# Rounding the turned products of the FFNs later and in a fixed order, bias rows issued earlier, upper token parts first, in a two-layer decoder trunk

## The chip, the cores and the metric

One core of one Trainium2 chip. The metric is the device time of one execution in microseconds (us); a kernel's time is the median of several runs. An engine has its own queue and works through it in order: PE (TensorE, matrix products), DVE (VectorE), ACT (ScalarE), POOL (GpSimd); SP (SyncE) here only issues DMAs.

## The reference

Two layers over 256 tokens of width 1024, batch 1, float32. Each layer has an FFN, a token mixer and another FFN. The first mixer is a gated linear recurrence, the second an attention with forget gates, whose keys, values and gates are made from the stream after the first layer. Cut to what matters here:

```python
def swiglu(x, w_gate, w_up, w_down):
    return (jax.nn.silu(x @ w_gate) * (x @ w_up)) @ w_down      # 1024 -> 2816 -> 1024

f = swiglu(rms_norm(h, ffn1_pre_g[layer]), ffn1_w_gate[layer], ffn1_w_up[layer], ffn1_w_down[layer])
h = h + 0.5 * rms_norm(f, ffn1_post_g[layer])
...
logits = logits + c[:, :, q0:end, None] - c[:, :, None, :end]   # c: running sum of log forget gates
```

There are four FFNs. In order of time they are called the first (first layer, ahead of the mixer), second (first layer, behind it), third (second layer, ahead of the attention) and fourth FFN here.

## The kernel before, in words

**Split operands.** To keep float32 accuracy, every operand of a large product is held as two parts: an upper part rounded by ACT (an activation with Copy into `fp32r`) and a lower part, the rest, subtracted by DVE. A product is then three matmuls: upper x upper, upper x lower, lower x upper (`mm3`, L183 to L185). For weights the parts are `whi` (L173) and `wlo` (L177), for tokens `xhi` and `xlo`, for the hidden activations of an FFN `hhi` (L527) and `hlo` (L528).

**Units and slots.** The weights come in units of 512 KB (1024 numbers in each of 128 partitions): one DMA on SP's queue into one of five `raw` buffers, one `whi` and one `wlo` into one of nine pairs of buffers. The 256 tokens are two halves of 128. A slot is one unit for one half: six matmuls of 512 columns. The first half runs some units ahead of the second (four in the middle of an FFN, eight at its end); a pair of weight buffers is free again when the second half has used it. Matmul results lie in four banks (`mm`).

**An FFN** has 66 units: 5 column blocks of 512 with 4 units of the gate and 4 of the up weights each, 4 units that hold both for the last 256 columns, and 22 units of the down weights. `proj_items` makes the units of the column blocks, `pair_items` the four mixed ones, `row_items` those of the down projection, which holds two banks for each half of the tokens.

**The path of a product.** When a half is done with an up block, ACT has `sil` (silu of the gate, L498) and DVE multiplies the up bank with it into `prod` (L507), which sets that bank free. There are 12 products in an FFN: ten of 512 columns, numbers 1 to 10, and two of 256, numbers 11 and 12. The down projection needs them with the hidden columns on the partitions, so each is turned: POOL copies `prod` into `pl` with the upper and the lower 16 bits of each number apart (L510), a DMA on SP's queue turns these 16-bit halves back into `prod`'s buffer (`hidden_T`, L517), POOL joins them into `pl` (L522), then ACT and DVE make `hhi` and `hlo` from `pl` (`parts`, L527 and L528). `prod` and `pl` have two buffers each.

**What sets the order.** PE's order is written out by hand. A step that is to come some slots later is put off with `defer(n, ...)`, which counts slots. For the other engines the framework sets the order by a schedule of its own; an instruction handed to `keep_in_program_order` stays where the program has it among those that are pinned so.

**The bias rows.** For the attention, the running sums of the forget gates (`crows` in DRAM, 16 heads x 256 keys) are spread over 128 partitions. For the second block of queries that is put together in DRAM (`bias1d`): `bias_rows(0)` issues on POOL's queue one transfer of 1 MB from DRAM to DRAM for the first 128 keys (`key_rows`, L952); then four times a quarter of the heads for the other 128 keys is loaded (`bp`, L952), masked on POOL (L948) and stored (`bias_part`, L969). All this is tied to the units of the third FFN by `ahead`, from 18 units before its end on.

Of the kernel before, what the change touches and what calls it, by code (L numbers as in the profile page):

```python
# [9 lines left out]
F32 = mybir.dt.float32  # L10
# [3 lines left out]
AF = mybir.ActivationFunctionType  # L14
ALU = mybir.AluOpType
AX = mybir.AxisListType

P = 128
# [7 lines left out]
NH = 16  # L26
# [17 lines left out]
def trunk_kernel(ctx: ExitStack, tc: tile.TileContext, A: dict, out: bass.AP):  # L44
    nc = tc.nc
# [28 lines left out]
    def tensor_work(n):  # L74
        pace["t"] += n * 0.445e-3
# [5 lines left out]
    def defer(n, fn):  # L81
        pend.append([n, fn])
# [98 lines left out]
    def mm3(ps, xh, xl, wh, wl, first, last):  # L181
        tensor_work(3 * wh.shape[1])
        nc.tensor.matmul(ps, xh, wh, start=first, stop=False)  # L183
        nc.tensor.matmul(ps, xh, wl, start=False, stop=False)  # L184
        nc.tensor.matmul(ps, xl, wh, start=False, stop=last)  # L185
# [205 lines left out]
    def proj_items(w, c0, nn, get_x, post, nk=8):  # L391

        kper = min(1024 // nn, 4)
        acc = {}

        for k0 in range(0, nk, kper):
            kn = min(kper, nk - k0)

            def fetch(k0=k0, kn=kn, pieces=1):
                return load_raw(w[k0 * P:(k0 + kn) * P, c0:c0 + nn].rearrange("(k p) n -> p k n", p=P), P, kn * nn, pieces)  # L400

            def prep(fetch=fetch, kn=kn):
                return split(fetch(), P, kn * nn)

            def work(t, u, k0=k0, kn=kn, i=len(items)):
                if i < OPEN:
                    if k0 + kn == nk:
                        post(t, first_acc[t][:, :nn])
                    return
                if k0 == 0:  # L410
                    acc[t] = mmbank()
                ps = acc[t][:, :nn]
                for j in range(kn):
                    k = k0 + j
                    mm3(ps, *get_x(t, k), u.hi[:, j * nn:(j + 1) * nn], u.lo[:, j * nn:(j + 1) * nn], k == 0, k == nk - 1)
                if k0 + kn == nk:
                    post(t, acc[t][:, :nn])
            if len(items) < OPEN:
                first_loads.append(fetch)
            items.append((prep, work))  # L420
# [54 lines left out]
    def ahead(i, fn):  # L475

        prep, work = items[i]

        def both():
            fn()  # L480
            return prep()
        items[i] = (both, work)

    def ffn_items(pool_of, wg, wu, wd, post_g, next_dests, last=False, normed=False):
# [17 lines left out]
        def post_up(c0, nn):  # L502
            def f(t, ps):
                hh, hl = hid_tiles(t)
                s = sil[t][:, :nn]
                pr = pool_of().tile([P, 512], F32, tag="prod", name=nm("prod"), bufs=2)
                nc.vector.scalar_tensor_tensor(pr[:, :nn], ps, rs[t][:, 0:1], s, ALU.mult, ALU.mult)  # L507
                halves = hpool.tile([P, 512], F32, tag="t1", name=nm("pl"), bufs=2).bitcast(U16)[:, :2 * nn]
                turned = pr.bitcast(U16)[:, :2 * nn].rearrange("p (a b) -> p a b", b=P)
                nc.gpsimd.tensor_copy(halves.rearrange("p (h f) -> p h f", h=2),  # L510
                                      pr[:, :nn].bitcast(U16).rearrange("p (f h) -> p h f", h=2))
                defer(1, lambda: hidden_T(halves, turned, hh, hl))

            def hidden_T(halves, turned, hh, hl):

                m, k0 = nn // P, c0 // P
                nc.sync.dma_start(turned, halves, transpose=True)  # L517
                hv = hh[:, k0:k0 + m, :].rearrange("p a b -> p (a b)")
                lv = hl[:, k0:k0 + m, :].rearrange("p a b -> p (a b)")

                def join():
                    nc.gpsimd.tensor_copy(halves.rearrange("p (f h) -> p h f", h=2),  # L522
                                          turned.rearrange("p (h a) b -> p h (a b)", h=2))

                def parts():
                    x = halves.bitcast(F32)
                    nc.scalar.activation(hv, x, AF.Copy)  # L527
                    nc.vector.tensor_tensor(lv, x, hv.bitcast(F32), ALU.subtract)  # L528
                defer(3, join)
                defer(6, parts)  # L530
            return f

        i0 = len(items)
# [417 lines left out]
    def key_rows(v, h0, nh, k):  # L951
        tc.keep_in_program_order(nc.gpsimd.dma_start(v, kv["rows"][h0:h0 + nh, k * P:(k + 1) * P].partition_broadcast(P)))  # L952
# [2 lines left out]

    def bias_rows(i):
        def f():
            if i == 0:
                key_rows(kv["bias1"][:, :, :P], 0, NH, 0)
            v = parts_of_bias[i] = pools["f"].tile([P, 512], F32, tag="sil", name=nm("bp"), bufs=2).rearrange(  # L960
                "p (a b) -> p a b", a=4)
            key_rows(v, 4 * i, 4, 1)
        return f
# [142 lines left out]
    for g in range(4):  # L1106
# [3 lines left out]
    ffn_items(lambda: pools["f"], A["ffn1_w_gate"][1], A["ffn1_w_up"][1], A["ffn1_w_down"][1], A["ffn1_post_g"][1],  # L1110
              std_dests(GI[("mix", 1)]))
    n_ffn3 = len(items)
    for i in range(4):
        ahead(n_ffn3 - 18 + 4 * i, bias_rows(i))
        ahead(n_ffn3 - 15 + 4 * i, bias_part(i))
# [340 lines left out]
```

## Time and profile before

| | |
|---|---|
| median of 3 runs | 994.34 us (993.0 to 996.06) |
| the profiled execution's own time | 991.57 us |
| its span, first to last instruction | 989.9 us |
| mean granted clock of TensorE | 0.992 |
| moved by DMA | 196.83 MB, 199 GB/s in the mean |
| read from HBM | 182.32 MB |

Busy time of an engine is the time in which its instructions ran, not counting those that issue DMAs or set registers. In a list of waits, "A <- B: total, times, longest" says how long A's engine stood still ahead of A until B had released it. In a timeline, each row has the start in us from the span's beginning, the duration, the engine, the line, the operation and the tiles it writes and reads, and in brackets how long the engine was idle before it and what ended that. PEld is the loading of weights into TensorE, which runs beside the matmuls. A line number is that of the kernel before; the changed kernel has the same statements five to six lines further down where the diff has added lines.

### The profile page before, as it was taken

To read this page: it belongs to the slowest core of one execution; us is meant where nothing else is said; L and a number is where in the kernel's file an instruction comes from. 1 tells how busy PE (TensorE), PEld (TensorE's weight loads), DVE (VectorE), ACT (ScalarE), POOL (GpSimd) and SP (SyncE) were. 2 spreads that over 40 slices of the span, in tenths; PEclk is the share of its full clock that TensorE was granted. 3 is DMA by queue.
4 is the path that set the end of the run, shared out by engine and by line. 5 is a ranking of instruction groups with operands and counts; after the bars stand their busy time and mean duration, and the time that the engine had idled before them with its cause. 6 is when DMAs were issued, how large, how long until landed. Compare 5 with 4: busy or idle time off the path is not lost. (4 is left out here: it accounts for less than half of the span.)

```text
span 989.9 us, 13061 instructions
## 1 busy us (share of the span) xinstructions
PE 963.7 (97%) x4687; PEld 800.0 (81%) x4687; DVE 627.9 (63%) x849; ACT 522.1 (53%) x749; POOL 201.7 (20%) x206
## 2 busy tenths in 40 slices
PE   9999979999999999999999999996999999999997
PEld 6888868888888888878899888875887788888785
DVE  6758655578997665554686455554487876565642
ACT  7546434558986554443565344433366865444431
POOL 2613230000001223330102132334020012323300
PEclk9999999999999999999999999997999999999999
DMA  8687876475437867766589578777764368777631
GB/s 290 209 265 206 262 225 206 137 210 164 127 107 226 227 191 224 221 212 207 117 218 297 160 216 208 222 222 230 219 222 140 107 193 234 203 215 237 209 123 43
DMA packets 142646, 196.83 MB, mean 199 GB/s; under 512 B 58798, under 2 KB 81686, under 8 KB 142454
## 3 DMA queue, kind: packets, MB, share of 16 engines
q1 hardware_dynamic: 139782, 188.96, 64.6%
q0 software_dynamic: 2192, 6.51, 2.2%
q8 instruction: 37, 0.61, 0.3%
q10 hardware_dynamic: 608, 0.53, 0.2%
q14 instruction: 27, 0.22, 0.1%
HBM read 182.32 MB, written 3.16 MB: 187 GB/s over the span
## 5 line engine op out<-in xcount | busy, mean ns | idle before, releaser
L177 DVE TENSOR_TENSOR wlo<-raw,whi 128x1024 fp32r<-128x1024 f32 (+5 forms) x329 | 414.0, 1272 | 159.1 <-ACT whi L173 156.1
L173 ACT ACTIVATE whi<-raw 128x1024 fp32r<-128x1024 f32 (+5 forms) x329 | 338.0, 1042 | 201.1 <-PE mm L185 137.9
L183 PE MATMUL mm<-whi,xhi 128*128 128x512 f32 (+1 forms) x768 | 300.0, 391 | 0.0
L185 PE MATMUL mm<-whi,xlo 128*128 128x512 f32 (+1 forms) x768 | 298.3, 388 | 0.3 <-DVE xlo L228 0.3
L184 PE MATMUL mm<-wlo,xhi 128*128 128x512 f32 (+1 forms) x768 | 298.3, 388 | 0.0
L183 PEld LDWEIGHTS mm<-whi,xhi 128*128 128x128 f32 x768 | 144.5, 188 | 30.9 <-issue 2.0
L185 PEld LDWEIGHTS mm<-whi,xlo 128*128 128x128 f32 x768 | 144.5, 188 | 30.6 <-DVE xlo L228 0.7
L184 PEld LDWEIGHTS mm<-wlo,xhi 128*128 128x128 f32 x768 | 144.5, 188 | 28.9 <-DVE wlo L177 0.3
L183 PE MATMUL mm<-whi,hhi 128*128 128x512 f32 x352 | 138.9, 395 | 17.7 <-DVE prod L507 17.7
L185 PE MATMUL mm<-whi,hlo 128*128 128x512 f32 x352 | 137.9, 392 | 0.0
L184 PE MATMUL mm<-wlo,hhi 128*128 128x512 f32 x352 | 137.9, 392 | 0.0
L527 ACT ACTIVATE hhi<-pl 128x512 fp32r<-128x512 f32 (+1 forms) x48 | 28.6, 596 | 178.8 <-POOL pl L522 178.8
L510 POOL COPY pl<-prod 128x1024 uint16<-128x1024 uint16 (+1 forms) x48 | 79.9, 1669 | 204.5 <-DVE prod L507 192.9
L528 DVE TENSOR_TENSOR hlo<-pl,hhi 128x512 fp32r<-128x512 f32 (+1 forms) x48 | 31.0, 646 | 135.5 <-ACT hhi L527 135.5
L183 PEld LDWEIGHTS mm<-whi,hhi 128*128 128x128 f32 x352 | 66.7, 190 | 33.9 <-DVE prod L507 20.3
L522 POOL COPY pl<-prod 128x1024 uint16<-128x1024 uint16 (+1 forms) x48 | 63.0, 1313 | 151.8 <-DMA prod<-pl 151.8
L185 PEld LDWEIGHTS mm<-whi,hlo 128*128 128x128 f32 x352 | 66.7, 189 | 14.0
L184 PEld LDWEIGHTS mm<-wlo,hhi 128*128 128x128 f32 x352 | 66.7, 190 | 13.6
L198 POOL TENSOR_SCALAR nv<-ss 128x1 f32<-128x1 f32 x22 | 9.7, 440 | 325.6 <-ACT junk L205 325.6
L507 DVE SCALAR_TENSOR_TENSOR prod<-mm,rstd,sil 128x512 f32<-128x512 f32 (+1 forms) x48 | 33.6, 701 | 1.5 <-PE mm L185 1.5
L498 ACT ACTIVATE sil<-mm,rstd 128x512 f32<-128x512 f32 (+1 forms) x48 | 30.7, 642 | 4.9 <-PE mm L185 3.3
L205 ACT ACTIVATE junk<-mm 128x512 bf16<-128x512 f32 x24 | 14.3, 594 | 32.7 <-PE mm L185 32.7
(211 smaller groups left out, 923.3 us busy)
## 6 DMA issues: line engine op xcount, KB each, us to landing
raw<-in_ffn_w_down_dram SPq DMA_DIRECT2D x88, 512.0 KB
raw<-in_ffn_w_up_dram SPq DMA_DIRECT2D x80, 512.0 KB
raw<-in_ffn_w_gate_dram SPq DMA_DIRECT2D x78, 512.0 KB
raw<-in_rg_w_in_dram SPq DMA_DIRECT2D x10, 504.0 KB
raw<-in_rg_w_out_dram SPq DMA_DIRECT2D x10, 504.0 KB
raw<-in_ffn_w_gate_dram SPq DMA_DIRECT2D x19, 256.0 KB
raw<-in_ffn_w_up_dram SPq DMA_DIRECT2D x16, 256.0 KB
raw<-in_rg_w_in_dram SPq DMA_DIRECT2D x8, 512.0 KB
```

Of the source, the lines that this page charges most:

```text
L173: up = nc.scalar.activation(hi[:parts, c:c + m], rawv[:, c:c + m], AF.Copy)
L177: nc.vector.tensor_tensor(lo[:parts, c:c + m], rawv[:, c:c + m], hi[:parts, c:c + m].bitcast(F32), ALU.subtract)
L183: nc.tensor.matmul(ps, xh, wh, start=first, stop=False)
L184: nc.tensor.matmul(ps, xh, wl, start=False, stop=False)
L185: nc.tensor.matmul(ps, xl, wh, start=False, stop=last)
L205: nc.scalar.activation(junk[:, :src.shape[1]], src, AF.Square, scale=f, accum_out=acc)
L498: nc.scalar.activation(s[:, :nn], ps, AF.Silu, scale=rs[t][:, 0:1])
L507: nc.vector.scalar_tensor_tensor(pr[:, :nn], ps, rs[t][:, 0:1], s, ALU.mult, ALU.mult)
L510: nc.gpsimd.tensor_copy(halves.rearrange("p (h f) -> p h f", h=2), pr[:, :nn].bitcast(U16).rearrange("p (f h) -> p h f", h=2))
L522: nc.gpsimd.tensor_copy(halves.rearrange("p (f h) -> p h f", h=2), turned.rearrange("p (h a) b -> p h (a b)", h=2))
L527: nc.scalar.activation(hv, x, AF.Copy)
L528: nc.vector.tensor_tensor(lv, x, hv.bitcast(F32), ALU.subtract)
```

## The change

It has four parts.

- In `proj_items` the six matmuls of a slot come in another order: for both slices of the unit the two products with the upper part of the tokens, then for both the one with the lower part.
- `hidden_T` is put off by two slots instead of one, and its DMA is pinned in program order.
- `parts` is put off by seven slots behind `hidden_T` instead of six, and its two instructions are pinned.
- The 1 MB transfer of the bias rows is issued 40 units before the end of the third FFN instead of 18, apart from the first quarter of the other rows.

```diff
@@ proj_items
                 ps = acc[t][:, :nn]
+                tensor_work(3 * kn * nn)
                 for j in range(kn):
-                    k = k0 + j
-                    mm3(ps, *get_x(t, k), u.hi[:, j * nn:(j + 1) * nn], u.lo[:, j * nn:(j + 1) * nn], k == 0, k == nk - 1)
+                    k, c = k0 + j, slice(j * nn, (j + 1) * nn)
+                    nc.tensor.matmul(ps, get_x(t, k)[0], u.hi[:, c], start=k == 0, stop=False)
+                    nc.tensor.matmul(ps, get_x(t, k)[0], u.lo[:, c], start=False, stop=False)
+                for j in range(kn):
+                    k, c = k0 + j, slice(j * nn, (j + 1) * nn)
+                    nc.tensor.matmul(ps, get_x(t, k)[1], u.hi[:, c], start=False, stop=k == nk - 1)
@@ ffn_items, post_up
-                defer(1, lambda: hidden_T(halves, turned, hh, hl))
+                defer(2, lambda: hidden_T(halves, turned, hh, hl))
 
             def hidden_T(halves, turned, hh, hl):
 
                 m, k0 = nn // P, c0 // P
-                nc.sync.dma_start(turned, halves, transpose=True)
+                keep = tc.keep_in_program_order
+                keep(nc.sync.dma_start(turned, halves, transpose=True))
...
                 def parts():
                     x = halves.bitcast(F32)
-                    nc.scalar.activation(hv, x, AF.Copy)
-                    nc.vector.tensor_tensor(lv, x, hv.bitcast(F32), ALU.subtract)
+                    keep(nc.scalar.activation(hv, x, AF.Copy))
+                    keep(nc.vector.tensor_tensor(lv, x, hv.bitcast(F32), ALU.subtract))
                 defer(3, join)
-                defer(6, parts)
+                defer(7, parts)
@@ bias_rows
         def f():
-            if i == 0:
-                key_rows(kv["bias1"][:, :, :P], 0, NH, 0)
             v = parts_of_bias[i] = ...
@@ behind the third FFN
     n_ffn3 = len(items)
+    ahead(n_ffn3 - 40, lambda: key_rows(kv["bias1"][:, :, :P], 0, NH, 0))
     for i in range(4):
         ahead(n_ffn3 - 18 + 4 * i, bias_rows(i))
         ahead(n_ffn3 - 15 + 4 * i, bias_part(i))
```

In the instruction streams, PE's sequence of result tiles is the same as before; only the order within slots differs.

## The prediction

> **What bounds the kernel now.** I read the page first, for which engine is full.
>
> ```profile
> PE 963.7 (97%) x4687; PEld 800.0 (81%) x4687; DVE 627.9 (63%) x849; ACT 522.1 (53%) x749; POOL 201.7 (20%) x206
> PEclk9999999999999999999999999997999999999999
> ```
>
> TensorE (PE) is busy for 963.7 of 989.9 us, and its clock falls in one slice. It is the bound, and only some 26 us are not matmul. An edit that adds no matmul can gain what PE waits, plus what it loses at a lower clock, and no more. So the next view is what PE itself waits for.
>
> ```profile
> engine line waited for: us in total, times, longest us
> PE mm L183 <- DVE prod L507: 17.7, 6, 9.3
> PE mm L185 <- DVE xlo L228: 0.3, 1, 0.3
> ```
>
> One cause holds 17.7 us in six waits: a matmul of the down projection waits for `prod` (L507) on VectorE (DVE), which reads the matmul bank that PE needs next. The product is short, so the question is what DVE stood behind. The waits of all engines name it.
>
> ```profile
> ACT hhi L527 <- POOL pl L522: 178.8, 48, 8.5
> POOL pl L522 <- DMA prod<-pl: 151.8, 47, 6.7
> DVE hlo L528 <- ACT hhi L527: 135.5, 41, 7.9
> ```
>
> This is the path of a turned product: transposing DMA, join on GpSimd (POOL), upper part `hhi` on ScalarE (ACT), lower part `hlo` on DVE. All 48 `hhi` make ACT stand still (3.7 us in the mean). Everything queued behind waits too: the rounding of weights (`whi`, then `wlo`), `sil`, `prod`. The timeline where the first FFN passes to its down projection shows one such wait reaching PE.
>
> ```profile
> 118.29 1.06 ACT L173 ACTIVATE whi<-raw 128x1024 fp32r<-128x1024 f32 x1 [0.28 <-DMA raw<-in_ffn_w_down_dram]
> 120.16 1.07 ACT L173 ACTIVATE whi<-raw 128x1024 fp32r<-128x1024 f32 x1 [0.80 <-DMA raw<-in_ffn_w_down_dram]
> 121.44 1.06 ACT L173 ACTIVATE whi<-raw 128x1024 fp32r<-128x1024 f32 x1 [0.21 <-DMA raw<-in_ffn_w_down_dram]
> 124.32 0.39 PE L185 MATMUL mm<-whi,xlo 128*128 128x512 f32 x1
> 125.44 1.32 POOL L522 COPY pl<-prod 128x1024 uint16<-128x1024 uint16 x1 [3.86 <-DMA prod<-pl]
> 126.80 0.63 ACT L527 ACTIVATE hhi<-pl 128x512 fp32r<-128x512 f32 x1 [4.29 <-POOL pl L522]
> 127.33 1.99 ACT L173 ACTIVATE whi<-raw 128x1024 fp32r<-128x1024 f32 x2
> 128.40 1.22 DVE L177 TENSOR_TENSOR wlo<-raw,whi 128x1024 fp32r<-128x1024 f32 x1 [0.26 <-ACT whi L173]
> 129.55 0.74 DVE L507 SCALAR_TENSOR_TENSOR prod<-mm,rstd,sil 128x512 f32<-128x512 f32 x1
> 130.34 0.64 PE L183 MATMUL mm<-whi,hhi 128*128 128x512 f32 x1 [4.96 <-DVE prod L507]
> ```
>
> The matmul whose result `prod` wants is over at 124.7. `prod` runs at 129.55, because `wlo` before it waited for a `whi` that stood behind `hhi`. PE is idle for 4.96 us. The third FFN (second layer, first FFN) has the longest wait, with a large GpSimd transfer in it.
>
> ```profile
> 656.73 0.50 PE L183 MATMUL mm<-whi,hhi 128*128 128x512 f32 x1 [0.18 <-DVE prod L507]
> 658.66 1.14 POOL L952 DMA_DIRECT2D bias1d<-crows  x1
> 667.29 1.32 POOL L522 COPY pl<-prod 128x1024 uint16<-128x1024 uint16 x1 [6.72 <-DMA prod<-pl]
> 668.64 0.63 ACT L527 ACTIVATE hhi<-pl 128x512 fp32r<-128x512 f32 x1 [8.47 <-POOL pl L522]
> 671.94 0.63 POOL L948 TENSOR_SCALAR_AFFINE_SELECT bp<-bp 128x512 f32<-128x512 f32 x1 [2.80 <-DMA bp<-crows]
> 674.46 0.42 ACT L527 ACTIVATE hhi<-pl 128x256 fp32r<-128x256 f32 x1 [4.24 <-POOL pl L522]
> 675.28 0.48 DVE L507 SCALAR_TENSOR_TENSOR prod<-mm,rstd,sil 128x256 f32<-128x256 f32 x1
> 675.82 0.79 PE L183 MATMUL mm<-whi,hhi 128*128 128x512 f32 x1 [9.26 <-DVE prod L507]
> 436.61 0.50 PE L183 MATMUL mm<-whi,hhi 128*128 128x512 f32 x1 [1.09 <-DVE prod L507]
> 929.44 0.50 PE L183 MATMUL mm<-whi,hhi 128*128 128x512 f32 x1 [1.69 <-DVE prod L507]
> ```
>
> ACT waits 8.47 us for one `hhi` and 4.24 us for the next, and the last product, behind both, leaves PE idle for 9.26 us. The last two rows are the second and the fourth FFN. The sixth wait is 17.7 - 4.96 - 9.26 - 1.09 - 1.69 - 0.18 = 0.5 us. After the two long ones PE also runs slowly, as the windows say (third count: PE; then the clock).
>
> ```profile
> 120.00:125.00 5.00, 5.00 (x24) 4.13 (x22) 3.22 (x3) 2.13 (x2) 1.58 (x1) 1.00 1.03 318
> 130.00:135.00 5.00, 4.66 (x13) 3.68 (x14) 3.39 (x4) 0.62 (x1) 3.45 (x2) 0.66 0.64 166
> 675.00:680.00 5.00, 4.18 (x10) 3.31 (x11) 3.27 (x4) 2.25 (x3) 2.37 (x3) 0.50 0.53 129
> ```
>
> A mean clock of 0.66 over 5 us is 3.4 us at half clock: 1.7 us lost. In the third FFN PE runs at 0.50 from 675.8 to about 680: 2.1 us lost.
>
> **The change part by part.** *Rounding later.* In the first FFN's ACT queue the product numbers 9 to 11 are `pl_218`, `pl_231`, `pl_237`; `whi` is a weight unit, `sil` the gate. Before:
>
> ```order
> L173 ACTIVATE whi_225_1183<-raw_224_1181 128x1024
> L527 ACTIVATE hhi_56_348<-pl_218_1152 128x512
> L173 ACTIVATE whi_228_1202<-raw_227_1200 128x1024
> L173 ACTIVATE whi_233_1224<-raw_232_1222 128x1024
> L498 ACTIVATE sil_235_1234<-mm_223_1168,rstd_36_284 128x256
> L173 ACTIVATE whi_240_1253<-raw_239_1251 128x1024
> ```
>
> And in the changed kernel:
>
> ```order
> L173 ACTIVATE whi_225_1183<-raw_224_1181 128x1024
> L173 ACTIVATE whi_228_1201<-raw_227_1199 128x1024
> L173 ACTIVATE whi_233_1224<-raw_232_1222 128x1024
> L503 ACTIVATE sil_235_1234<-mm_223_1167,rstd_36_284 128x256
> L173 ACTIVATE whi_240_1250<-raw_239_1248 128x1024
> L533 ACTIVATE hhi_56_348<-pl_218_1150 128x512
> ```
>
> `hhi` of product 9 moves back by three `whi`. Over all 48 the move is three `whi`, with one of four and four of two. The transposing DMAs on SP's queue keep their place, except that 7 of the 48 let one more weight load go ahead, at the ends of the FFNs. So `hhi` gets the whole move as slack. What three `whi` are in time, where ACT runs at PE's pace:
>
> ```profile
> 684.24 1.06 ACT L173 ACTIVATE whi<-raw 128x1024 fp32r<-128x1024 f32 x1 [1.66 <-PE mm L185]
> 686.96 1.06 ACT L173 ACTIVATE whi<-raw 128x1024 fp32r<-128x1024 f32 x1 [1.66 <-PE mm L185]
> ```
>
> They are 2.72 us apart, so the move is worth 8.2 us, against a mean wait of 3.7 and a longest of 8.5. I expect almost all of the 178.8 us of ACT's waits to go. DVE at the end of the third FFN, products 10 to 12 (`prod_1113`, `prod_1120`, `prod_1135`), before:
>
> ```order
> L507 SCALAR_TENSOR_TENSOR prod_1120_5871<-mm_1106_5800,rstd_821_4321,sil_1119_5869 128x256
> L177 TENSOR_TENSOR wlo_1130_5909<-raw_1128_5906,whi_1129_5908 128x1024
> L528 TENSOR_TENSOR hlo_975_5162<-pl_1114_5852,hhi_974_5161 128x512
> L177 TENSOR_TENSOR wlo_1133_5933<-raw_1131_5930,whi_1132_5932 128x1024
> L528 TENSOR_TENSOR hlo_960_5089<-pl_1121_5873,hhi_959_5088 128x256
> L507 SCALAR_TENSOR_TENSOR prod_1135_5950<-mm_1122_5878,rstd_854_4446,sil_1134_5948 128x256
> ```
>
> Now:
>
> ```order
> L512 SCALAR_TENSOR_TENSOR prod_1120_5871<-mm_1106_5800,rstd_821_4321,sil_1119_5869 128x256
> L177 TENSOR_TENSOR wlo_1125_5886<-raw_1123_5883,whi_1124_5885 128x1024
> L534 TENSOR_TENSOR hlo_960_5089<-pl_1101_5783,hhi_959_5088 128x512
> L177 TENSOR_TENSOR wlo_1130_5909<-raw_1128_5906,whi_1129_5908 128x1024
> L177 TENSOR_TENSOR wlo_1133_5932<-raw_1131_5929,whi_1132_5931 128x1024
> L512 SCALAR_TENSOR_TENSOR prod_1135_5950<-mm_1122_5875,rstd_854_4446,sil_1134_5948 128x256
> ```
>
> The last product no longer stands behind the lower parts of products 10 and 11, whose joins came late, but only behind that of product 9. All that was waited for there goes: 4.96 + 1.7 (first FFN), 9.26 + 2.1 + 0.18 (third), 1.09, 1.69, 0.5: **21.5 us** is the most that this can give.
>
> What is late next: in the first FFN `prod` 10 can't start before its matmul is over at 124.7 and takes 0.74, while PE wants the bank at 125.4 (130.34 - 4.96): at least 0.1 us stays. The `wlo` ahead of it needs a `whi` that can follow the one of 121.44 at once, or must wait for one more load as those before it did; at their widest spacing (118.29 to 120.16, 1.87) it starts at 123.3, and 1.06 for itself, 0.1 and 1.22 for `wlo` and 0.74 for `prod` give 126.5. So 0.1 to 1.1 stays, and I take 0.6, the middle. Of the three small waits I leave 0.2 each, by the 0.18 that the third FFN shows where nothing stood ahead: 0.6. The pin adds no instruction; PE reads these parts only some ten units on in its order.
>
> *Bias rows.* POOL's queue at the third FFN's end (`bias1d` is the 1 MB transfer, `bp` a quarter of the second block's rows). Before:
>
> ```order
> L510 COPY pl_1114_5852<-prod_1113_5850 128x1024
> L952 DMA bias1d_2950<-crows_2948 2048x1x128
> L952 DMA bp_1115_5855<-crows_2948 128x4x128
> L522 COPY pl_1114_5852<-prod_1113_5850 128x2x512
> L510 COPY pl_1121_5873<-prod_1120_5871 128x512
> L948 AFFINE_SELECT bp_1115_5855<-bp_1115_5855 128x512
> ```
>
> Now:
>
> ```order
> L515 COPY pl_1114_5853<-prod_1113_5851 128x1024
> L958 DMA bp_1115_5855<-crows_2948 128x4x128
> L954 AFFINE_SELECT bp_1115_5855<-bp_1115_5855 128x512
> L528 COPY pl_1114_5853<-prod_1113_5851 128x2x512
> L515 COPY pl_1121_5873<-prod_1120_5871 128x512
> ```
>
> The large transfer now stands behind the fourth product, but the join of product 10 (L528) moved behind the mask, which waits for `bp`. Product 12 writes the buffer that this join reads.
>
> ```profile
> bias1d<-crows POOLq DMA_DIRECT2D x1, 1024.0 KB, 11.8
> bp<-crows POOLq DMA_DIRECT2D x4, 256.0 KB, 6.0
> DMA to landing us min/median/max: 4.6/7.4/12.2
> ```
>
> `bp` is issued at 658.7 and lands L later; mask 0.63, join 1.32 and product 0.48 follow: PE gets the bank at 658.7 + L + 2.5. It wants it at 666.6 (675.82 - 9.26). With the median 6.0 of `bp` the wait is 0.6; with 4.6, none; with 12.2, which had the 1 MB ahead of it, 6.8. I take 0.9, a little over the median's, and leave product 10's own 0.18. At its new place the 1 MB delays a transposition by some 3.5 us (6.72 here against 3.2, the mean of the 47: 151.8 / 47); the 8.2 us of slack hide it, and without them ACT would wait those 3.5 us.
>
> The Trainium skill (Trainium Kernel Development and Optimization, Key Constraints) speaks against this part: DMAs issued from SP, ACT and POOL run on the same 16 DMA engines and interleave, so that another place moves the collision and does not remove it. The trace agrees: behind the 1 MB, POOL waited 6.72 us for the transposition. That is the second rival.
>
> *Upper parts first.* The same six matmuls a unit, in another order: no instruction more. It can save the one wait for `xlo`, 0.3 us, and cost as much where `wlo` is read one matmul earlier; I take 0.
>
> Sum: -21.5 + 0.6 (first FFN) + 0.6 (three small waits) + 0.9 + 0.2 (third FFN) = **-19.2 us**. The profiled execution took 991.57 (span 989.9), so 972.4; the median of the runs is 2.8 higher, 994.34, and gives **975.1**.
>
> **The rivals.** (1) *The third FFN keeps its wait, now behind the mask.* If `bp` lands like the slowest, 6.8 us of waiting and 2.1 of slow clock remain: 8.9 instead of 0.9, so 983.1. For it: the join really stands behind the mask; against: the 12.2 had the 1 MB in front.
> (2) *The collision moves.* At the fourth product of the third FFN the transposition is 3.5 us late and PE waits as long, plus 1.7 at half clock: 980.3. Against: 48 waits of ACT, 3.7 us in the mean, reached PE only six times, all near a down projection.
> (3) *Loads are late next.* The `whi` at 121.44 waits for its load. If that decides, the first FFN keeps 6.7 us instead of 0.6: 981.2.
> (4) *Slower: the two `pl` buffers are held longer.* Product 11 may be copied (L515) only when `hlo` of product 9 is done, three `whi` later, and POOL puts it behind the join of product 10. SP's transposition waits for the copy, and the down weights queue behind it. It decides if SP is held longer than five raw buffers cover, 5 x 2.72 = 13.6 us. If it did, each of four down projections would start as the first one does now, 4.96 + 1.7, in all 26.6 against 21.5 gained: 999.4. Against: the join is a few us late, not 13.6.
> (5) *Nothing moves:* DVE's products are held by something else all along. Against: the chain above has no gap.
>
> **How the numbers follow.** A difference of 0.3% is 3.0 us, about what can be told from no change. Chances: forecast 0.74, (1) 0.11, (2) 0.05, (3) 0.04, (4) 0.03, (5) 0.03. Faster: 0.74 + 0.11 + 0.05 + 0.04 = 0.94; same 0.03; slower 0.03. The low end is the whole 21.5 us, and 2.8 more if what sets the median above the profiled run is the same waiting: 970.0. The high end takes in rivals (1) to (3): 984.0.
>
> **What would show it.** Right: PE's waits for `prod` fall from 17.7 to about 2.4 us, ACT's for the join from 178.8 to below 30, no half-clock stretch at the down projections, PE busy time nearly unchanged but for the slow stretches. Rival (1): a PE wait of several us in the third FFN, with the mask on POOL just ahead of the join. (2): one near the fourth product. (4): SP's transposition of product 11 followed by late loads, and `whi` waiting for them. The prediction is wrong if the ACT waits go and PE's time does not fall.

## The result and the profile after

| | before | after |
|---|---|---|
| median on the same chip, 4 runs each | 994.59 us (993.0 to 996.06) | 968.39 us (968.24 to 968.57) |
| ratio of the two | | 0.9737 [0.972, 0.9754] |
| the profiled execution's own time | 991.57 us | 968.35 us |
| its span | 989.9 us | 966.6 us |

The changed kernel is 26.2 us faster, 6.7 us below the forecast of 975.1 and 1.6 us below the range's low end. Direction and place were right; the size lay outside the range. The page of the changed kernel, busy time and clock:

```profile
PE 958.6 (99%) x4687; PEld 798.1 (83%) x4687; DVE 640.1 (66%) x849; ACT 526.1 (54%) x749; POOL 193.4 (20%) x206
PEclk9999999999999999999999999999999999999999
```

PE's busy time fell only by 5.1 us, the span by 23.3: what went was idle time and the slice at a lower clock. The list of PE's waits in the changed kernel (total, times, longest):

```profile
PE tr L127 <- PEq L1446: 0.8, 1, 0.8
PE gt L767 <- issue: 0.5, 1, 0.5
```

The row for `prod` (17.7 us in six) is gone altogether, and so is the one for `xlo`. The waits of the path behind it, from the list of all engines:

```profile
ACT hhi L533 <- POOL pl L528: 7.3, 3, 2.8
POOL pl L528 <- DMA prod<-pl: 173.3, 47, 11.0
ACT whi L173 <- PE mm L420: 113.2, 79, 3.3
```

POOL waits for the transpositions even longer than before (173.3 against 151.8 us). But ACT no longer stands still behind it: 7.3 us in 3 waits instead of 178.8 in 48. Now it mostly waits for PE to free weight buffers, that is, it runs ahead. The windows at the first FFN's passage (third count: PE, then the clock):

```profile
125.00:130.00 5.00, 5.00 (x24) 4.14 (x23) 3.40 (x4) 2.55 (x3) 1.78 (x2) 1.00 0.99 302
130.00:135.00 5.00, 5.00 (x24) 4.14 (x23) 2.23 (x3) 2.94 (x4) 2.37 (x3) 1.00 0.60 203
```

PE is full and at full clock where it had 0.39 us of work and then a mean clock of 0.66. The timeline there shows the order that was to be brought about:

```profile
115.87 1.06 ACT L173 ACTIVATE whi<-raw 128x1024 fp32r<-128x1024 f32 x1 [3.40 <-DMA raw<-in_ffn_w_down_dram]
121.76 0.39 PE L420 MATMUL mm<-whi,xlo 128*128 128x512 f32 x1
122.36 0.75 DVE L512 SCALAR_TENSOR_TENSOR prod<-mm,rstd,sil 128x512 f32<-128x512 f32 x1
122.57 1.36 POOL L528 COPY pl<-prod 128x1024 uint16<-128x1024 uint16 x1 [6.52 <-DMA prod<-pl]
124.48 0.39 PE L185 MATMUL mm<-whi,xlo 128*128 128x512 f32 x1
125.39 0.39 PE L183 MATMUL mm<-whi,hhi 128*128 128x512 f32 x1
125.88 0.61 ACT L533 ACTIVATE hhi<-pl 128x512 fp32r<-128x512 f32 x1
```

The join of product 9 comes at 122.57, after 6.52 us of waiting on POOL; ACT does not wait for it, since its `hhi` runs 3.3 us later. Product 10 begins 0.21 us after its last matmul is over (122.15), and the bank is free at 123.11, 2.28 us before PE takes it at 125.39. The same matmul began at 130.34 in the kernel before.

**Where the time came from.** Both profiles hold the same 4,687 matmuls, so each one's start can be set against its like. The difference grows in seven steps; in no other place does it change by more than 0.4 us. (In its first microseconds the changed kernel falls 0.16 us behind.)

| place (start in the profile before) | gained, us | priced in the prediction, us |
|---|---|---|
| the start of the kernel | -0.16 | 0 |
| first FFN, 130.34, with the half clock behind it | 6.84 | 4.96 + 1.7 |
| first FFN, 142.29 | 0.84 | 0.5 |
| second FFN, first matmul that reads `xlo`, 308.97 | 0.47 | 0 |
| second FFN, 436.61 | 1.38 | 1.09 |
| third FFN, 656.73 | 0.47 | 0.18 |
| third FFN, 675.82, with the half clock | 11.53 | 9.26 + 2.1 |
| fourth FFN, 929.44 | 1.98 | 1.69 |
| sum | 23.35 | 21.5 |

991.57 - 23.35 = 968.22; the profiled run took 968.35.

### The profile page after: what moved, and what is told of

It is laid out like the page before. It is cut to its first block, busy times and chain, and to the rows that moved or that the text cites. A ratio compares the mean times of both kernels' runs of the same rounds, so it can differ in the third digit from the quotient of the medians.

```text
span 966.6 us, 13061 instructions
## 1 busy us (share of the span) xinstructions
PE 958.6 (99%) x4687; PEld 798.1 (83%) x4687; DVE 640.1 (66%) x849; ACT 526.1 (54%) x749; POOL 193.4 (20%) x206
## 4 chain that ended last, share of the span: by engine, by line
PE 96%; DVE 1%; issue 1%; ACT 1%; POOLq 0%; POOL 0%; DVEq 0%; ACTq 0%
PE mm L416 16%; PE mm L417 15%; PE mm L420 15%; PE mm L183 13%; PE mm L185 13%; PE mm L184 13%; PE mm L1027 2%; PE gt L767 2%; PE mm L1296 1%; PE mm L190 1%; PE mm L191 1%; PE mm L192 1%; PE gt L214 1%; PE tr L127 0%; ACT pe L1172 0%
## 5 line engine op out<-in xcount | busy, mean ns | idle before, releaser
L416 PE MATMUL mm<-whi,xhi 128*128 128x512 f32 x656 | 256.7, 391 | 0.0
L417 PE MATMUL mm<-wlo,xhi 128*128 128x512 f32 x656 | 255.5, 390 | 0.0
L420 PE MATMUL mm<-whi,xlo 128*128 128x512 f32 x656 | 202.2, 389 | 0.0
L420 PEld LDWEIGHTS mm<-whi,xlo 128*128 128x128 f32 x656 | 123.1, 188 | 26.0 <-DVE xlo L228 0.2
L416 PEld LDWEIGHTS mm<-whi,xhi 128*128 128x128 f32 x656 | 123.2, 188 | 25.7 <-issue 0.7
L417 PEld LDWEIGHTS mm<-wlo,xhi 128*128 128x128 f32 x656 | 123.2, 188 | 25.1 <-DVE wlo L177 0.3
L185 PE MATMUL mm<-whi,hlo 128*128 128x512 f32 x352 | 137.0, 389 | 0.0
L184 PE MATMUL mm<-wlo,hhi 128*128 128x512 f32 x352 | 136.9, 389 | 0.0
L528 POOL COPY pl<-prod 128x1024 uint16<-128x1024 uint16 (+1 forms) x48 | 69.6, 1449 | 173.3 <-DMA prod<-pl 173.3
L515 POOL COPY pl<-prod 128x1024 uint16<-128x1024 uint16 (+1 forms) x48 | 64.1, 1335 | 175.8 <-DVE prod L512 107.0
L184 PEld LDWEIGHTS mm<-wlo,hhi 128*128 128x128 f32 x352 | 66.1, 188 | 13.7
L185 PEld LDWEIGHTS mm<-whi,hlo 128*128 128x128 f32 x352 | 66.1, 188 | 13.7
L534 DVE TENSOR_TENSOR hlo<-pl,hhi 128x512 fp32r<-128x512 f32 (+1 forms) x48 | 40.1, 835 | 5.1 <-ACT hhi L533 5.1
L183 PE MATMUL mm<-whi,xhi 128*128 128x512 f32 (+1 forms) x112 | 42.8, 382 | 0.0
L185 PE MATMUL mm<-whi,xlo 128*128 128x512 f32 (+1 forms) x112 | 42.5, 379 | 0.0
```

Of the source, the lines that this page charges most:

```text
L416: nc.tensor.matmul(ps, get_x(t, k)[0], u.hi[:, c], start=k == 0, stop=False)
L417: nc.tensor.matmul(ps, get_x(t, k)[0], u.lo[:, c], start=False, stop=False)
L420: nc.tensor.matmul(ps, get_x(t, k)[1], u.hi[:, c], start=False, stop=k == nk - 1)
L534: keep(nc.vector.tensor_tensor(lv, x, hv.bitcast(F32), ALU.subtract))
```

## The experiments

Each kernel ran beside the kernel before on the same chip, whose median was 993.45, 992.75 and 992.66 us (13 runs each, 990.36 to 995.96 over all) in the three sets. "Theory" in the expectations is that of the prediction: slack for `hhi` frees DVE's products, and so PE.

### Which of the four parts does it

**The later, pinned rounding alone.** The changed kernel with the old order of the matmuls and the old place of the bias transfer.

```diff
 # changed kernel
-    ahead(n_ffn3 - 40, lambda: key_rows(kv["bias1"][:, :, :P], 0, NH, 0))
 # bias_rows(0) issues it again, 18 units before the end; proj_items uses mm3 again
```

> The kernel before with the rounding later and pinned, but with the 1 MB bias transfer and PE's order in a slot as before. Theory: what freed PE is that the products no longer stand behind the parts of turned products; only the third FFN should keep a wait, because the last product needs the buffer that the join of product 10 reads, and that join ended at 668.6 where PE wants the bank at 666.6: about 2.5 us, plus 0.3 that each wait costs beyond its idle time, and 0.5 us that the order in a slot saves is missing. So 968.4 + 2.8 + 0.5 = 971.7 us. Rival A (the bias transfer is what makes the long wait): the third FFN keeps its 11.5 us, so about 980. Rival B (each part is needed): well above 980.

Measured: 968.57 us (968.55 to 972.21, 4 runs), ratio 0.976 [0.9736, 0.9784]. PE waits for no `prod`. This part is nearly the whole gain. The 3.1 us that the theory left to the other parts are not there in three of the four runs.

**The change without the early bias transfer.**

```diff
 # changed kernel
+            if i == 0:
+                key_rows(kv["bias1"][:, :, :P], 0, NH, 0)
-    ahead(n_ffn3 - 40, lambda: key_rows(kv["bias1"][:, :, :P], 0, NH, 0))
```

> The changed kernel with the 1 MB bias transfer back at 18 units before the third FFN's end. Theory: a wait of 2 to 3 us in the third FFN, no half clock, 968.4 + 2.8 = 971.2 us. Rival A: the 11.5 us of the third FFN come back, about 980. Rival C (the moved transfer does nothing once the rounding is later): 968.4.

Measured: 969.24 us (968.43 to 970.74, 4 runs), ratio 0.9759 [0.9739, 0.978]. The profiled run (968.55) has no wait of PE for `prod`. Its matmuls stand 0.3 us behind those of the change from the first microseconds on, and no further behind in the third FFN: in this execution the early transfer is worth nothing beside the later rounding. Two of the four runs took 1.6 and 2.4 us more than the profiled run of the change. That the transfer's place is the cause is not shown, since kernels that issue it early have such runs too (970.75 and 970.86 us below).

**The early bias transfer alone**, on the kernel before.

```diff
 # kernel before
-            if i == 0:
-                key_rows(kv["bias1"][:, :, :P], 0, NH, 0)
+    ahead(n_ffn3 - 40, lambda: key_rows(kv["bias1"][:, :, :P], 0, NH, 0))
```

> The kernel before with only the 1 MB bias transfer moved to 40 units before the third FFN's end. Theory: the wait of the third FFN shrinks to what the second and fourth show (1.4 to 2.0 us of lost time), so 9.5 to 10 us are gained, the waits of the other three stay: about 984.8 us by the timed median. Rival (the transfer has no part in it): 994.6. Rival (its new place disturbs the fourth product): more than 985, with a PE wait near 592 us.

Measured: 990.72 us (987.34 to 996.57, 10 runs), ratio 0.9979 [0.9958, 1.0]; the expectation missed. Its list of PE's waits:

```profile
PE mm L183 <- DVE prod L507: 14.5, 6, 5.1
```

And the two in the third FFN, from the timeline:

```profile
659.57 0.80 PE L183 MATMUL mm<-whi,hhi 128*128 128x512 f32 x1 [2.63 <-DVE prod L507]
673.72 0.79 PE L183 MATMUL mm<-whi,hhi 128*128 128x512 f32 x1 [2.85 <-DVE prod L507]
```

The third FFN's long wait has become two shorter ones, and each drags a stretch at half clock behind it; the first FFN's stays. While `hhi` has no slack, the path only finds another join to wait for.

**The change with PE's old order within slots.**

```diff
 # changed kernel, proj_items, shortened
-                tensor_work(3 * kn * nn)
-                # upper part for both slices, then lower part
+                for j in range(kn):
+                    k = k0 + j
+                    mm3(ps, *get_x(t, k), u.hi[:, j * nn:(j + 1) * nn], u.lo[:, j * nn:(j + 1) * nn], k == 0, k == nk - 1)
```

> The changed kernel with PE's order within a slot as before. Theory: one wait of PE for the lower part of the tokens comes back at the start of the second FFN, 0.3 us of idle time that costs 0.35 to 0.5: 968.75 us, within 968.5 to 969.0. Rival (the order is worth nothing): 968.4. Rival (it saves more than one wait): 970 or more.

Measured: 968.59 us (968.48 to 970.75, 4 runs), ratio 0.9763 [0.9741, 0.9784]. One row comes back in PE's list:

```profile
PE mm L185 <- DVE xlo L228: 0.3, 1, 0.3
```

By the starts of the matmuls it costs 0.45 us. The difference of the medians, 0.2 us, is too small to be told from the runs alone. The profiled execution is the longest of the four, 970.75 us, and its other 1.9 us are lost within the first 10 us: from 5 to 10 us PE has 13 matmuls at work where the change has 22, in the same 4.91 us of busy time. The run of 970.86 us below lost 2.0 us at the same place.

### The pin or the slots

**The pins alone**: turning put off by one slot and parts by six, as before; bias transfer and matmul order as before.

```diff
 # kernel before, plus keep(...) around the DMA, hhi and hlo
-                nc.sync.dma_start(turned, halves, transpose=True)
+                keep(nc.sync.dma_start(turned, halves, transpose=True))
-                    nc.scalar.activation(hv, x, AF.Copy)
-                    nc.vector.tensor_tensor(lv, x, hv.bitcast(F32), ALU.subtract)
+                    keep(nc.scalar.activation(hv, x, AF.Copy))
+                    keep(nc.vector.tensor_tensor(lv, x, hv.bitcast(F32), ALU.subtract))
```

> The kernel before with the transposing DMA and the two roundings pinned, but put off by as many slots as before (1 and 6). In the instruction streams the upper parts then stand two weight roundings later than before instead of three. Theory: two roundings are 5.4 us of slack against ACT's waits of 3.7 us in the mean and 8.5 at most; the first, second and fourth FFN lose nothing or a few tenths, the third keeps 3 us: about 972 to 974 us. Rival (three are needed): waits of more than a us in several FFNs, 978 or more.

Measured: 974.16 us (972.27 to 975.59, 4 runs), ratio 0.9812 [0.9788, 0.9836]. `hhi` mostly stands two `whi` later than before (a few of them one or three). One wait is left, at the third FFN's end; the timeline:

```profile
645.88 1.14 POOL L953 DMA_DIRECT2D bias1d<-crows  x1
656.98 1.31 POOL L523 COPY pl<-prod 128x1024 uint16<-128x1024 uint16 x1 [9.19 <-DMA prod<-pl]
658.33 0.48 DVE L507 SCALAR_TENSOR_TENSOR prod<-mm,rstd,sil 128x256 f32<-128x256 f32 x1 [3.83 <-POOL pl L523]
658.87 0.50 PE L183 MATMUL mm<-whi,hhi 128*128 128x512 f32 x1 [1.97 <-DVE prod L507]
660.32 0.63 PE L185 MATMUL mm<-whi,hlo 128*128 128x512 f32 x1
```

This is another wait than any in the kernel before: product 12 writes the buffer that the join of product 10 must have read, and that join waits 9.19 us for a transposition behind the 1 MB. No `hhi` is in it.

**The slots alone**: both numbers raised, nothing pinned.

```diff
 # kernel before
-                defer(1, lambda: hidden_T(halves, turned, hh, hl))
+                defer(2, lambda: hidden_T(halves, turned, hh, hl))
-                defer(6, parts)
+                defer(7, parts)
```

> The kernel before with the two larger slot counts (2 and 7) but without any pin. Its instruction streams are row for row those of the kernel before on all five engines. Theory (the pins are what moves the roundings; the slot counts alone do nothing): like the kernel before, 990.9 to 996.6 us, median near 993.5, PE waits for prod near 18 us in six waits, and the size of those waits differs from execution to execution. Rival (the later slots do it): near 970.

Measured: 992.82 us (989.34 to 995.06, 10 runs), ratio 1.0 [0.9984, 1.0016]. The waits:

```profile
PE mm L183 <- DVE prod L507: 17.9, 5, 9.0
```

The scheduler put every instruction where it was before: the streams of all engines are the same, row for row. A slot number that is not pinned moves nothing here.

**The roundings pinned, the DMA not.**

```diff
 # changed kernel
-                keep(nc.sync.dma_start(turned, halves, transpose=True))
+                nc.sync.dma_start(turned, halves, transpose=True)
```

> The changed kernel without the pin of the transposing DMA; the two roundings stay pinned. Theory: the pin of the roundings is what moves them, and the rows of ACT's queue are as in the changed kernel, so the time is 968.4 us, 968.0 to 969.2, and ACT's waits for the join stay below 15 us. Rival: the DMA's pin counts (weight loads pass it): 970 us or more, with ACT's waits for the join above 30 us.

Measured: 968.29 us (968.18 to 968.44, 4 runs), ratio 0.9739 [0.9723, 0.9755]. The streams of all engines are those of the change, row for row: the pin that counts is that of `hhi` and `hlo`.

### How much slack, and when it is too much

**Three slots instead of seven**, pinned: 42 of the 48 `hhi` stand one `whi` later than before, six at their old place.

```diff
 # changed kernel
-                defer(7, parts)
+                defer(3, parts)
```

> The changed kernel with the two roundings put off by 3 slots behind the transposition instead of 7, pinned as now. In the instruction streams the upper parts stand 0 or 1 weight rounding later than in the kernel before. Theory (what counts is the slack): 2.7 us are less than ACT's mean wait of 3.7, so waits of ACT for the join of 50 to 90 us remain and PE waits again at the FFNs' ends: 978 to 988 us. Rival (that the place is fixed is what counts, not how late it is): 969.

Measured: 972.58 us (971.87 to 977.22, 4 runs), ratio 0.9808 [0.9777, 0.9838]. Both sizes that were expected failed; the time lies between. The waits of PE and of ACT:

```profile
PE mm L183 <- DVE prod L512: 3.0, 3, 1.6
```

```profile
ACT hhi L533 <- POOL pl L528: 47.7, 26, 7.0
```

ACT still waits 47.7 us, and PE sees 3.0 of them. One unit of slack (2.72 us) is less than the mean wait of 3.7, yet takes 83% of the gain, (992.75 - 972.58) / (992.75 - 968.39). I read it so, without having shown it, that what reaches PE is the tail of the waits and not their mean.

**Twelve slots.** `hhi` stands five to six `whi` later than before (one of them four, one seven).

```diff
 # changed kernel
-                defer(7, parts)
+                defer(12, parts)
```

> The changed kernel with the parts put off by 12 slots instead of 7: hhi five to six weight units later than before instead of three, so each pl buffer is held two to three units (5.4 to 8.2 us) longer, and the last two transpositions of each FFN stand three to four weight loads later on SP's queue. Theory: three units of slack were enough already and five raw buffers (13.6 us) still cover the loads: 968 to 969.5 us, no PE wait for prod. Rival, the fourth of the prediction: the buffers are held too long already, the copy into pl waits, and at each down projection PE waits some us: 975 us or more.

Measured: 968.49 us (968.38 to 968.61, 4 runs), ratio 0.9741 [0.9725, 0.9757]. More slack than three units brings nothing and costs nothing.

**Eighteen slots.** `hhi` stands eight to nine later (one seven, one ten), the transpositions up to seven loads later on SP's queue.

```diff
 # changed kernel
-                defer(7, parts)
+                defer(18, parts)
```

> The changed kernel with the parts put off by 18 slots: hhi eight to nine weight units later than before; pl is held some 24 us longer than before, nearly the time between two products (4 + 4 units of 2.72 us = 21.8 us a block of both halves), and the transpositions stand three to seven weight loads later on SP's queue. Theory: now the fourth rival's point is passed: the copy into pl waits for the lower part of two products before, the turned product comes late, prod's two buffers are not free and PE waits: 972 to 1000 us, with waits of POOL's copy for hhi or hlo of several us at most products. Rival: the order still covers it (schedule moved the transpositions along): 968 to 970 us.

Measured: 990.84 us (987.33 to 992.76, 10 runs), ratio 0.9971 [0.9954, 0.9987]: nearly the whole gain is lost again, and it begins where the prediction's fourth rival saw it, at the `pl` buffers. POOL's list of waits and the timeline of the first FFN:

```profile
POOL pl L515 <- DVE hlo L534: 202.3, 37, 12.8
```

```profile
134.80 0.69 DVE L534 TENSOR_TENSOR hlo<-pl,hhi 128x512 fp32r<-128x512 f32 x1
135.55 1.97 POOL L515 COPY pl<-prod 128x1024 uint16<-128x1024 uint16 x1 [3.45 <-DVE hlo L534]
141.01 1.32 POOL L528 COPY pl<-prod 128x1024 uint16<-128x1024 uint16 x1 [3.49 <-DMA prod<-pl]
142.37 0.48 DVE L512 SCALAR_TENSOR_TENSOR prod<-mm,rstd,sil 128x256 f32<-128x256 f32 x1 [3.77 <-POOL pl L528]
143.00 0.76 PE L183 MATMUL mm<-whi,hhi 128*128 128x512 f32 x1 [5.84 <-DVE prod L512]
```

Read upwards from PE: it waits 5.84 us for the last product, which waits for the join, which waits for the transposition, which could start only after the copy, which waited for `hlo` of two products before. The buffers are held too long. What stops PE is `prod`, not a missing weight: the rival had the right buffer and named the wrong successor (SP's loads).

### The collision with the 1 MB transfer

**The transfer four times**, 40, 32, 24 and 18 units before the end.

```diff
 # changed kernel
-    ahead(n_ffn3 - 40, lambda: key_rows(kv["bias1"][:, :, :P], 0, NH, 0))
+    for back in (40, 32, 24, 18):
+        ahead(n_ffn3 - back, lambda: key_rows(kv["bias1"][:, :, :P], 0, NH, 0))
```

> The changed kernel with the 1 MB bias transfer issued four times (40, 32, 24 and 18 units before the third FFN's end; the same rows each time). Theory: with three weight roundings of slack a transposition that is 3.5 us late reaches no one, so 968.4 to 969.5 us, and ACT's waits for the join stay under 25 us. Rival (the collision is only moved by the change, and costs where it lands): about 3.5 us and half a clock stretch of 1.7 for each of the three extra transfers, up to 984.

Measured: 968.25 us (967.81 to 969.98, 4 runs), ratio 0.976 [0.9735, 0.9785]. POOL's waits for transpositions rise from 173.3 to 181.9 us; PE has no wait for `prod`.

**The pins alone with the early transfer**: does it cure the wait that the pins alone left?

```diff
 # changed kernel, mm3 order as before
-                defer(2, lambda: hidden_T(halves, turned, hh, hl))
+                defer(1, lambda: hidden_T(halves, turned, hh, hl))
-                defer(7, parts)
+                defer(6, parts)
```

> The pins alone (turning put off by one slot, parts by six, as before) with the 1 MB bias transfer issued 40 units before the third FFN's end; PE's order as before. The pins alone ran 974.16 us and lost 4.07 us at the third FFN's end: 2.0 of waiting and a stretch at half clock, where the join of product 10 had waited 9.2 us for its transposition behind the 1 MB. Theory: that collision is its cause and is not hidden by a slack of two weight units; with the 1 MB earlier it goes: 974.2 - 4.1 = 970.1 us, 969.3 to 971, no PE wait for prod above 0.5 us. Rival: the third FFN's last products wait for the join in any case (the early transfer alone brought 2 us, not 7): 973 to 975 us, with a PE wait of 1.5 us or more left in the third FFN.

Measured: 968.77 us (968.61 to 970.86, 4 runs), ratio 0.9749 [0.973, 0.9767]. It is 5.4 us below the pins alone (in another set, where the median of before was 0.8 us lower), and 0.5 below the range expected: I had taken the 4.07 us that one profiled run lost from the median of its kernel, 974.16, and not from that run's own 972.27, which gives 968.2. Product 12 in its timeline:

```profile
657.11 1.33 POOL L523 COPY pl<-prod 128x1024 uint16<-128x1024 uint16 x1
658.48 0.48 DVE L507 SCALAR_TENSOR_TENSOR prod<-mm,rstd,sil 128x256 f32<-128x256 f32 x1 [1.82 <-POOL pl L523]
```

It still waits 1.82 us for the join, but PE loses only some 0.3 us there. So the early transfer is worth nothing that can be told for sure on the kernel before (0 slack), 5.4 us with two units of slack, and with three 0.85 us by the medians (969.24 against 968.39), none of it in the third FFN of the profiled run. The parts of the change are not independent, and their gains do not add.

All together, by the place of `hhi` against the kernel before:

| kernel | `hhi` later by, in `whi` | median, us | PE waits for `prod` | ACT waits for the join |
|---|---|---|---|---|
| slots alone | 0 | 992.82 | 17.9 | 181.9 |
| parts at 3 | 0 to 1 | 972.58 | 3.0 | 47.7 |
| pins alone | 2 | 974.16 | 2.0 | 7.7 |
| pins, early transfer | 2 | 968.77 | none | 8.3 |
| the change | 3 | 968.39 | none | 7.3 |
| parts at 12 | 5 to 6 | 968.49 | none | none |
| parts at 18 | 8 to 9 | 990.84 | 17.4 | none |

The pins alone and parts at 3 also differ in the place of the 1 MB, which costs the former 5.4 us.

## What of the prediction held, and where it failed

**What held.** The bound (PE's waits for `prod` and the half clock behind them), the chain (join, `hhi`, `whi`, `wlo`, `prod`), and the cure (three units of slack against a longest wait of 8.5 us) are shown: the roundings alone bring 968.57, the slots without the pins nothing, and the waits in between go with the slack. Of ACT's 178.8 us 7.3 are left, below the 30 forecast. That the pin "adds no instruction" holds too (13,061 in both profiles).

**What failed is the size, by three terms.** The forecast lies 6.7 us too high: 2.3 + 1.9 + 2.8 = 7.0, less 0.2 by which the changed kernel's median lies above 991.57 - 23.35 = 968.22, and 0.1 of rounding.

1. *The 2.3 us that were to be left: nothing was.* Three steps are wrong. In the first FFN: "`prod` 10 can't start before its matmul is over at 124.7". That matmul was the last one ahead of the gap, and it writes another bank. Product 10's own last matmul is over at 122.15 in the changed kernel, where the one that I took begins at 124.48; so the product had 2.28 us to spare, not 0.1 to 1.1 too few. The `wlo` ahead of it, which the upper bound put at 124.5 to 125.7, was through at 122.44 (and the terms of that bound add up to 126.4, not 126.5). The source of a bank has to be sought by its tile, not by what stands next to the gap. In the small waits: 0.2 each, "by the 0.18 that the third FFN shows where nothing stood ahead". The parts of an earlier product did stand ahead there, as the first rows below show: ACT waited 4.32 us for a join, DVE 3.06 us for that `hhi`, and one `wlo` later product 10 came. So the 0.18 was the tail of the same wait. In the third FFN, too: "`bp` is issued at 658.7". That was the time at which the 1 MB was issued in the kernel before, when POOL itself was late behind product 10 (`bp` followed at 659.72):

```profile
653.17 0.63 ACT L527 ACTIVATE hhi<-pl 128x512 fp32r<-128x512 f32 x1 [4.32 <-POOL pl L522]
653.84 0.69 DVE L528 TENSOR_TENSOR hlo<-pl,hhi 128x512 fp32r<-128x512 f32 x1 [3.06 <-ACT hhi L527]
655.93 0.75 DVE L507 SCALAR_TENSOR_TENSOR prod<-mm,rstd,sil 128x512 f32<-128x512 f32 x1
659.72 0.86 POOL L952 DMA_DIRECT2D bp<-crows  x1
```

In the changed kernel, the same place:

```profile
643.81 0.75 DVE L512 SCALAR_TENSOR_TENSOR prod<-mm,rstd,sil 128x512 f32<-128x512 f32 x1 [0.35 <-PE mm L420]
645.68 0.78 POOL L958 DMA_DIRECT2D bp<-crows  x1
647.01 0.39 PE L183 MATMUL mm<-whi,hhi 128*128 128x512 f32 x1
652.57 0.63 POOL L954 TENSOR_SCALAR_AFFINE_SELECT bp<-bp 128x512 f32<-128x512 f32 x1 [6.11 <-DMA bp<-crows]
653.37 2.13 POOL L528 COPY pl<-prod 128x1024 uint16<-128x1024 uint16 x1 [0.17 <-DMA prod<-pl]
655.54 0.49 DVE L512 SCALAR_TENSOR_TENSOR prod<-mm,rstd,sil 128x256 f32<-128x256 f32 x1 [1.25 <-POOL pl L528]
656.53 0.39 PE L183 MATMUL mm<-whi,hhi 128*128 128x512 f32 x1
```

Product 10 now waits for its own matmul alone (0.35 us) and is over at 644.56, 2.45 us before PE wants its bank. `bp` was issued 2.99 us behind the matmul that wants that bank (656.73 in the kernel before; the 658.7 lies 1.9 us behind it), and now 1.33 us ahead of its like (647.01). It landed within 6.9 us, not 6.0, and the join took 2.13, not 1.32; the last product is over at 656.03 all the same, 0.5 us before PE wants its bank. The 0.9 was the right mechanism reckoned from a time that the change itself moves.

2. *"21.5 us is the most that this can give": it gave 23.35.* The table of the steps shows it: each of the four small waits cost 0.29 us more than its listed idle, 1.2 us in all, and each of the two long ones 0.16 us. Idle time is counted from the listed end of the last matmul, 0.39 us after its start, though the next one would start 0.23 us after it; and the first one behind the wait takes some 0.1 us longer than the others. In the second FFN before:

```profile
435.12 0.39 PE L185 MATMUL mm<-whi,hlo 128*128 128x512 f32 x1
436.61 0.50 PE L183 MATMUL mm<-whi,hhi 128*128 128x512 f32 x1 [1.09 <-DVE prod L507]
436.94 0.40 PE L184 MATMUL mm<-wlo,hhi 128*128 128x512 f32 x1
```

And after:

```profile
427.13 0.39 PE L185 MATMUL mm<-whi,hlo 128*128 128x512 f32 x1
427.36 0.39 PE L183 MATMUL mm<-whi,hhi 128*128 128x512 f32 x1
427.59 0.39 PE L184 MATMUL mm<-wlo,hhi 128*128 128x512 f32 x1
```

From L185 to L184 it is 1.82 us before and 0.46 after: 1.36 for a wait listed as 1.09. The other 0.5 us is the order of the matmuls, taken as 0 between a gain of 0.3 and a like cost: it gained 0.47, since the wait for `xlo` went and no wait took its place. The two half-clock stretches, 1.72 and 2.11 us by the starts of the matmuls, were priced well (1.7 and 2.1).

3. *The 2.8 us added because the median of before lies above its profiled run.* They were carried over as if they belonged to the kernel; the changed kernel's median lies 0.04 us above its profiled run. The low end allowed that they were the same waits; the forecast should have done so. Kernels with the waits spread over some 5 us (990.36 to 995.96 for before, 989.34 to 995.06 for the slots alone, 987.33 to 992.76 for parts at 18), and the change, the DMA unpinned and parts at 12 over 0.2 to 0.3. That fits waits that vary from execution to execution, but does not show it: the other five kernels without a wait for `prod` have one or two runs of four that are 1.5 to 3.7 us above their fastest, and the two of those runs that were profiled, 970.75 and 970.86, lost 1.9 and 2.0 us in the first 10 us. The two profiles of the order before (991.57 and, for the slots alone, 991.76) are both of short executions, so what makes the long ones stays open.

**The rivals.** (1) The join does stand behind the mask and product 12 waits 1.25 us for it, but 0.5 us remain; it did not decide. (2) The collision did move, and it was larger than priced. The join behind the 1 MB at its new place, and its `hhi`:

```profile
580.40 1.14 POOL L958 DMA_DIRECT2D bias1d<-crows  x1
592.52 1.34 POOL L528 COPY pl<-prod 128x1024 uint16<-128x1024 uint16 x1 [10.98 <-DMA prod<-pl]
593.89 0.63 ACT L533 ACTIVATE hhi<-pl 128x512 fp32r<-128x512 f32 x1 [2.80 <-POOL pl L528]
```

POOL waits 10.98 us, 7.8 above the mean of 3.2 where I put 3.5. The slack leaves 2.80 for ACT, and PE has no wait for `prod`, not even with four such transfers. The Trainium skill (Trainium Kernel Development and Optimization, Key Constraints) says that DMAs issued from SP, ACT and POOL run on the same 16 DMA engines and interleave; the prediction took from it that another place moves the collision and does not remove it, and these rows agree. It cost nothing because the slack took up all but 2.80 us of it. (3) Loads were late at times (one `whi` waits 3.40 us for its load at 115.87), but nothing of it reached PE: ACT and DVE had caught up when product 10 came at 122.36. (4) True in kind, false here: seven and twelve slots are short of its point, eighteen are past it, at 22.5 us (990.84 against 968.39) where I priced 26.6. (5) Fell with the first experiment.

## What to carry to other kernels

A step that waits in an in-order queue is cured by putting it behind as many units as cover its longest wait, here three of 2.72 us (two were enough only with the 1 MB out of the way); up to six cost nothing, and eight or nine held the `pl` buffers so long that nearly the whole gain went. Put off a step in a scheduled program only with a look at the stream that comes out, since a number that the scheduler overrides changes nothing. When a wait is taken out of a sum, reckon all later times anew from what PE wants, find the source of a bank by its tile, and measure a wait's price from start to start of the matmuls around it.

## What was not expected of the hardware

Whether a wait is followed by half clock does not go by its length alone. The first kernel is the early bias transfer alone, the second parts at 18, both in the fourth FFN:

```profile
928.85 0.68 PE L183 MATMUL mm<-whi,hhi 128*128 128x512 f32 x1 [1.93 <-DVE prod L507]
929.33 0.63 PE L184 MATMUL mm<-wlo,hhi 128*128 128x512 f32 x1
```

```profile
929.32 0.47 PE L183 MATMUL mm<-whi,hhi 128*128 128x512 f32 x1 [2.57 <-DVE prod L512]
929.62 0.40 PE L184 MATMUL mm<-wlo,hhi 128*128 128x512 f32 x1
```

After 1.93 us the matmuls come at 0.43 us each, after 2.57 us at 0.23. In all profiles here, every wait of 2.63 us and more was followed by the slow pace, none of 1.77 us and less, and those between went either way. The Trainium skill (TensorE: Matmul & The Clock Gate, Why this matters for your kernels) warns of idle gaps over some 3 us; the runs here show the loss from 1.93 us on, so the shorter gaps count too. What decides in between can be read from the traces' records of the granted clock. In each profile that has such stretches it changes only on a grid of 3.413 us: ahead of the kernel's end, the stretches at half clock last 3.41, 6.83 or 10.24 us, and from the start of the first one of parts at 18 (139.15) to the start of its third (675.04) it is 157 times 3.413. What counts, as far as the waits here show, is how much of a wait falls into one period of this grid. The 1.93 us lie in one period. The 2.57 us are cut by its edge into 0.89 and 1.69. Over all waits of PE for `prod` in these profiles, those with 1.93 us or more in one period were followed by half clock, and those with at most 1.77 were not. So two waits of one length can differ in price: in the fourth FFN the 1.93 us cost 3.8 us against the changed kernel, and 2.00 us in the profile of the slots alone, cut into 1.15 and 0.85, cost 2.3.

And a transposition for which POOL waited 3.2 us in the mean in the kernel before made it wait 10.98 us behind a 1 MB transfer of another queue in the changed one.
